# A hybrid decoder trunk whose list scheduler plays the program on another machine model

## The chip, the cores and the metric

The kernel runs on one core of a Trainium2 chip. The metric is device time in microseconds (us), the median of several runs. The engines are called as in the profile: PE is the tensor engine (PEld its weight loads), DVE the vector engine, ACT the scalar engine, POOL the GpSimd engine, SP the engine that issues most transfers.

## The reference

Two layers work on x of 256 tokens by 2048 features, in float32. A layer computes (cut from the reference):

```
h = rmsnorm(x, norm_mix[l])
fq, fk, fv, ff, gq, gk, gv, gg, gr, lg, lx = split(h @ w_in[l])        # 2048 x 5144
fox = softmax attention, 8 heads of 64, causal, with a cumulative forget bias from ff; then rmsnorm
gla = gated linear attention, 4 heads, chunked, decay from gr; rmsnorm per head, times silu(gg)
lru = rg_lru(causal_depthwise_conv(lx)) * gelu(lg); then rmsnorm
x = x + concat([fox, gla, lru]) @ w_out[l]                             # 2048 x 2048
h = rmsnorm(x, norm_ffn[l])
x = x + (silu(h @ w_gate[l]) * (h @ w_up[l])) @ w_down[l]              # 2048 x 5632 twice, 5632 x 2048
```

At the end one more rmsnorm gives the output, again 256 x 2048.

## The kernel before

Every product with a weight matrix is done in split form: a weight block of 128 x 1024 lands in a buffer `raw` (three of 1 MB), ACT casts it to the high part `wh` (L217 or L262), DVE subtracts to get the low part `wl` (L218 or L263), and PE multiplies high by high, high by low and low by high. There are four `wh` and four `wl` buffers, so the casts can run a few blocks ahead. `group` (L173 on) computes with tokens on the partitions, with the products in L200, L201 and L203 and the last blocks in L191 to L193; it does the output projection, called op, and the down projection, called dn. `group_T` (L224 on) computes with features on the partitions, L239 for the 512-column product and L240 for the 256-column one; it does lx, lg, gqk, fq, fk and the gate and up projections, called gu. `sum_T` (L281, L282) brings a result of these out of PSUM. Six PSUM buffers hold the results, two more (`aux`) hold everything small: transposes `tp`, softmax scores `fs`, transposed probabilities `pp`, attention outputs `fo`.

The mixers are written as generators. While a projection runs over its blocks, after each block it calls `next(steps)`, which emits a step of the mixer whose inputs are ready: conv taps (L483), the scans (L505), the chunk levels of the gated linear attention (masked copies in L684), the norm of the recurrent branch (L774), the tables `nb00` (L796) and `ck1` (L797) of the forget bias. The softmax runs beside the output projection: PE scores `fs` (L821), DVE subtracts the bias and takes the maximum (L837, L840, L841), ACT takes exp (L843), PE flips (`pp`, L852), ACT copies (`pT`, L854), PE multiplies with the values (`fo`, L863), DVE divides (L867), ACT squares (L871), DVE and POOL make the norm (L154, L156), DVE scales (L873), PE transposes (`tp`, L165), and ACT and DVE write the parts of `mt0` (L169, L170). The output projection reads the four quarters of its input in the order `mt2`, `mt3` (recurrent branch), `mt1` (linear attention), `mt0` (softmax), so the softmax has three quarters of the first half of the projection to run beside. The `final` function at the end adds the last products (L402), squares (L421), multiplies by the gain (L422), and scales by the norm (L431 on ACT, L433 on DVE) before the output is stored.

What the program text says is not yet the order of the queues. A list scheduler takes all instructions with what each waits for, plays the program on a model of the machine, and at each point gives an engine the ready instruction of highest priority; priority is the order of the text, but for stretches marked `tc.high_priority()` (the casts) or `tc.high_priority(SOONEST)` (the `sum_T` evacuations and the additions to x). What comes out is one fixed queue for each engine, worked in order on the chip. Which instruction is "ready" at a point is decided by the times of the model alone, so another model gives other queues.

## Time and profile before

| | us |
|---|---|
| time, median of 3 runs | 2082.35 (2082.15 to 2082.68) |
| profiled execution, its own time | 2081.86 |
| span of the profiled execution | 2080.1 |
| PE busy | 2063.2 |
| DVE busy | 1339.7 |
| ACT busy | 1108.6 |
| POOL busy | 12.9 |

The span is the stretch that the profile covers; the time has the ends around it. "Busy" of PE is a share of time in which a matmul is in its pipeline by a model of their ends, so it says that PE is fed, and not that it is at its peak. The granted clock is given by the profile as a share of 2.4 GHz. Names in the rows are those of the program; `op<-wh,mt` reads: result op, from wh and mt.

### The profile page before, as it was taken

What the parts mean: (1) busy time and instruction counts of PE and PEld (TensorE: products, weight loads), DVE (VectorE), ACT (ScalarE), POOL (GpSimd) and SP (SyncE); (2) the same over time, 40 slices, a digit from 0 to 9 for tenths busy, and PEclk for the clock granted to TensorE, in tenths of its full rate; (3) what the DMA queues carried; (4) which work ended last, traced back from release to release, by engine and by line L of the source; (5) the groups of instructions that cost most, each with busy time, mean ns of one, the idle gap of its engine ahead of it and who ended that gap; (6) DMA issues with size and microseconds to landing.
All of it is one profiled execution on the core that took longest, in us unless ns stands there. A gap on an engine that the chain in (4) does not pass through costs nothing.

```text
span 2080.1 us, 30286 instructions
## 1 busy us (share of the span) xinstructions
PE 2063.2 (99%) x11948; PEld 1865.3 (90%) x11948; DVE 1339.7 (64%) x1770; ACT 1108.6 (53%) x1557; POOL 12.9 (1%) x20
## 2 busy tenths in 40 slices
PE   9999999999999999999999999999999999999998
PEld 7899888999998899998898998889999888999987
DVE  7887856666655465655578878666665555565654
ACT  6875555554543345544458665555455444554543
POOL 0000000000000000000000000000000000000000
PEclk9999999999999999999999999999999999999999
DMA  7456545666666666666665565566666666666664
GB/s 277 151 190 194 196 147 198 202 200 199 200 199 204 205 201 200 199 201 202 201 196 161 185 193 182 162 202 198 200 199 199 200 204 205 201 199 201 202 203 162
DMA packets 302702, 406.66 MB, mean 196 GB/s; under 512 B 12208, under 2 KB 196960, under 8 KB 302432
## 3 DMA queue, kind: packets, MB, share of 16 engines
q1 hardware_dynamic: 297808, 401.47, 59.3%
q10 hardware_dynamic: 4752, 3.26, 0.5%
q8 instruction: 93, 1.52, 0.3%
q14 instruction: 49, 0.40, 0.1%
HBM read 402.57 MB, written 2.11 MB: 195 GB/s over the span
## 4 chain that ended last, share of the span: by engine, by line
PE 93%; DVE 3%; ACT 2%; issue 1%; DMA 0%; SPq 0%; ACTq 0%; POOLq 0%; DVEq 0%
PE gu L239 30%; PE gu L240 15%; PE dn L203 7%; PE dn L200 7%; PE dn L201 7%; PE lx L239 3%; PE op L201 2%; PE op L200 2%; PE op L203 2%; PE lx L240 1%; PE fq L239 1%; PE lg L239 1%; PE fk L239 1%; PE gqk L239 1%; DVE wl L218 1%
## 5 line engine op out<-in xcount | busy, mean ns | idle before, releaser
L239 PE MATMUL gu<-x,wh 128*128 128x512 f32 x2816 | 914.4, 382 | 0.0
L263 DVE TENSOR_TENSOR wl<-raw,wh 128x1024 fp32r<-128x1024 f32 (+1 forms) x465 | 566.1, 1220 | 371.9 <-ACT wh L262 371.8
L240 PE MATMUL gu<-x,wl 128*128 128x256 f32 x2816 | 739.3, 273 | 0.0
L262 ACT CAST wh<-raw 128x1024 fp32r<-128x1024 f32 (+1 forms) x465 | 485.4, 1047 | 456.9 <-PE gu L239 364.1
L239 PEld LDWEIGHTS gu<-x,wh 128*128 128x128 f32 x2816 | 519.6, 189 | 64.8
L240 PEld LDWEIGHTS gu<-x,wl 128*128 128x128 f32 x2816 | 539.6, 192 | 9.3
L218 DVE TENSOR_TENSOR wl<-raw,wh 128x1024 fp32r<-128x1024 f32 (+2 forms) x288 | 352.5, 1226 | 274.0 <-ACT wh L217 273.8
L217 ACT CAST wh<-raw 128x1024 fp32r<-128x1024 f32 (+2 forms) x288 | 300.8, 1047 | 331.2 <-PE dn L203 207.3
L200 PE MATMUL dn<-wh,ht 128*128 128x512 f32 x632 | 239.9, 380 | 0.0
L201 PE MATMUL dn<-wl,ht 128*128 128x512 f32 x632 | 239.5, 379 | 0.0
L203 PE MATMUL dn<-wh,ht 128*128 128x512 f32 x632 | 188.0, 379 | 0.0
L201 PEld LDWEIGHTS dn<-wl,ht 128*128 128x128 f32 x632 | 119.5, 189 | 16.9
L203 PEld LDWEIGHTS dn<-wh,ht 128*128 128x128 f32 x632 | 119.4, 189 | 16.9
L200 PEld LDWEIGHTS dn<-wh,ht 128*128 128x128 f32 x632 | 119.5, 189 | 16.8
L281 ACT COPY half<-gu 128x256 f32<-128x256 f32 x176 | 65.3, 371 | 45.7 <-PE gu L239 41.2
L239 PE MATMUL lg<-xt,wh 128*128 128x512 f32 x256 | 87.5, 394 | 1.4 <-DVE lg L282 1.4
L239 PE MATMUL lx<-xt,wh 128*128 128x512 f32 x256 | 87.3, 394 | 1.1 <-DVE xt L170 1.1
L200 PE MATMUL op<-wh,mt 128*128 128x512 f32 x224 | 87.1, 389 | 0.0
L201 PE MATMUL op<-wl,mt 128*128 128x512 f32 x224 | 86.0, 384 | 0.0
L240 PE MATMUL lx<-xt,wl 128*128 128x256 f32 x256 | 68.5, 279 | 0.0
L240 PE MATMUL lg<-xt,wl 128*128 128x256 f32 x256 | 67.2, 273 | 0.0
L203 PE MATMUL op<-wh,mt 128*128 128x512 f32 x224 | 67.0, 380 | 0.0
(300 smaller groups left out, 2313.3 us busy)
## 6 DMA issues: line engine op xcount, KB each, us to landing
raw<-in_w_gate SPq DMA_DIRECT2D x176, 512.0 KB, 3.5
raw<-in_w_up SPq DMA_DIRECT2D x176, 512.0 KB, 4.5
raw<-in_w_down SPq DMA_DIRECT2D x176, 512.0 KB, 4.8
raw<-in_w_in SPq DMA_DIRECT2D x55, 1024.0 KB, 5.0
raw<-in_w_out SPq DMA_DIRECT2D x64, 512.0 KB, 4.8
raw<-in_w_in SPq DMA_DIRECT2D x17, 512.0 KB, 3.6
raw<-in_w_in SPq DMA_DIRECT2D x16, 528.0 KB, 3.7
raw<-in_w_in SPq DMA_DIRECT2D x16, 520.0 KB, 3.9
```

Of the source, the lines that this page charges most:

```text
L200: T.matmul(out, hi, turns(wh[:, c]), start=k == 0, stop=False)
L201: T.matmul(out, hi, turns(wl[:, c]), start=False, stop=False)
L203: T.matmul(inturn(ps[i][h][:, :segs[i][1]]), lo, turns(wh[:, c]), start=False, stop=k == nk - 1)
L217: A.copy(wh, raw[:, j:j + jn, :tot])
L218: V.tensor_tensor(wl, raw[:, j:j + jn, :tot], f(wh), op=ALU.subtract)
L239: both = lambda: T.matmul(ps[i].rearrange("p (a t u) -> p a t u", a=2, u=2), wh[:, c], turns(xk), start=k == 0, stop=k == KT - 1)
L240: low = lambda: T.matmul(inturn(ps[i][:, 0:S]), wl[:, c], turns(xk[:, 0]), start=False, stop=False)
L262: A.copy(wh[:, js], raw[:, rs, :])
L263: V.tensor_tensor(wl[:, js], raw[:, rs, :], f(wh[:, js]), op=ALU.subtract)
L281: A.copy(two(c), halves_of(ps[:, S:]))
```

## The change

One argument is added where the program is built: the scheduler plays the program on a model that keeps time lines, in place of the default model. What the kernel computes, its instructions, buffers and priorities are as before. Of PE's 11,730 rows 1,552 stand at another place, of DVE's 1,772 rows 364, of ACT's 1,492 rows 227, of SP's 725 rows 3, and of POOL's none.

```
-    with tile.TileContext(nc) as tc:
+    with tile.TileContext(nc, schedule_with_timeline_sim=True) as tc:
```

The first place is the softmax of layer 1 on PE. `fs_2889` and `fs_2890` are the last two score tiles, `op0_...` the four result tiles of the output projection, `mt3` and `mt1` its earlier inputs, `mt0` the softmax's result. Before, the scores are followed by products of the projection (24 rows stand where the dots are; 12 more follow between pp and fo, 24 between fo and tp, 12 between the tp):

```order
L203 MATMUL op0_0_1_1_2708<-wh_2873,mt3_109 128x512
L821 MATMUL fs_2889<-fk_2183,fq_2182 128x256
L821 MATMUL fs_2890<-fk_2183,fq_2182 128x256
L821 MATMUL fs_2889<-fk_2183,fq_2182 128x256
L821 MATMUL fs_2890<-fk_2183,fq_2182 128x256
L200 MATMUL op0_0_0_0_2705<-wh_2918,mt3_109 128x512
...
L852 MATMUL pp_2950<-cst_80,pt_2895 128x128 x4
L852 MATMUL pp_2957<-cst_80,pt_2905 128x128 x4
L200 MATMUL op0_0_0_0_2705<-wh_2967,mt1_2454 128x512
```

Now the same stretch of PE's queue, from the last product ahead of `fs_2890` to the last flip:

```order
L203 MATMUL op0_0_1_1_2708<-wh_3056,mt1_2454 128x512
L821 MATMUL fs_2890<-fk_2183,fq_2182 128x256 x2
L852 MATMUL pp_2950<-cst_80,pt_2895 128x128 x4
L852 MATMUL pp_2957<-cst_80,pt_2905 128x128 x2
L863 MATMUL fo_2983<-fv_1952,pT_2864 128x64 x2
L863 MATMUL fo_2983<-fv_1952,pT_2871 128x64 x2
L863 MATMUL fo_2983<-fv_1952,pT_2864 128x64 x2
L863 MATMUL fo_2983<-fv_1952,pT_2871 128x64 x2
L863 MATMUL fo_2983<-fv_1952,pT_2955 128x64 x2
L852 MATMUL pp_2957<-cst_80,pt_2905 128x128 x2
```

The products with `mt3` and `mt1` now all stand ahead of `fs_2890`; three more pairs of fo and eight transposes tp follow the rows shown, and then the first product with `mt0`. Before, 72 products stood between `fs_2890` and that product; now none does, and 7 stand between `fs_2889` and `fs_2890`.

The second place is DVE beside the projection fq of layer 1. `wl_2270` and `wl_2292` are the low parts of two of its weight blocks. Before:

```order
L797 TENSOR_TENSOR ck1_1966<-ck1_1966,cst_80 128x1024
L263 TENSOR_TENSOR wl_2270<-raw_2241,wh_2269 128x1024
L263 TENSOR_TENSOR wl_2292<-raw_2289,wh_2291 128x1024
L684 COPY_PREDICATED at_1642<-msk_85,gx_2210 128x256x2
L774 SCALAR_TENSOR_TENSOR mt2_108<-hs_110,vec_83,mt2_108 128x256 x4
```

Now, from the same addition to the same cast:

```order
L797 TENSOR_TENSOR ck1_1966<-ck1_1966,cst_80 128x1024
L263 TENSOR_TENSOR wl_2270<-raw_2241,wh_2269 128x1024
L774 SCALAR_TENSOR_TENSOR mt2_108<-hs_110,vec_83,mt2_108 128x256 x3
L796 TENSOR_TENSOR nb00_1968<-ck0_1965,cst_80 128x1024
L774 SCALAR_TENSOR_TENSOR mt2_108<-hs_110,vec_83,mt2_108 128x256
L684 COPY_PREDICATED at_1642<-msk_85,gx_2210 128x256x2
L774 SCALAR_TENSOR_TENSOR mt3_109<-hs_110,vec_83,mt3_109 128x256 x2
L263 TENSOR_TENSOR wl_2292<-raw_2289,wh_2291 128x1024
```

The second cast now stands behind six L774, the table nb00 (L796) and the two masked copies.

The third place is DVE beside the projection lg of layer 1: `lg0` is its result as it is brought out of PSUM, `xc` the conv taps, `hs` the scan. Before:

```order
L263 TENSOR_TENSOR wl_940<-raw_910,wh_939 128x1024
L505 SCALAR_TENSOR_TENSOR hs_110<-av_543,ti_542 128x256 x2
L263 TENSOR_TENSOR wl_969<-raw_966,wh_968 128x1024
L282 TENSOR_TENSOR lg0_869<-lg00_0_659,half_870 128x256
L282 TENSOR_TENSOR lg0_869<-lg00_1_660,half_873 128x256
L505 SCALAR_TENSOR_TENSOR hs_110<-av_543,ti_542 128x256 x2
```

Now:

```order
L263 TENSOR_TENSOR wl_940<-raw_910,wh_939 128x1024
L483 SCALAR_TENSOR_TENSOR xc_885<-xp_645,vec_83,xc_885 128x256 x2
L263 TENSOR_TENSOR wl_969<-raw_966,wh_968 128x1024
L282 TENSOR_TENSOR lg0_869<-lg00_0_659,half_870 128x256
L505 SCALAR_TENSOR_TENSOR hs_110<-av_543,ti_542 128x256 x3
L282 TENSOR_TENSOR lg0_869<-lg00_1_660,half_873 128x256
```

The first evacuation and the conv taps now stand ahead of the scans; before, two scans stood ahead of the first evacuation and the taps came behind the last one.

## Rows read from the trace of the kernel before

**Rows 1.** Busy times of the page: engine, us, share of the span, instructions.

```profile
PE 2063.2 (99%) x11948; PEld 1865.3 (90%) x11948; DVE 1339.7 (64%) x1770; ACT 1108.6 (53%) x1557; POOL 12.9 (1%) x20
```

**Rows 2.** Timeline of PE in the down projection: start us, length us, instruction.

```profile
2060.71 0.38 PE L192 MATMUL dn<-wl,ht 128*128 128x512 f32 x1
2060.93 0.38 PE L193 MATMUL dn<-wh,ht 128*128 128x512 f32 x1
```

**Rows 3.** PE's waits: line waited with <- line waited for: us, times, longest.

```profile
PE lg L239 <- DVE lg L282: 1.4, 2, 0.7
PE gp L490 <- DVE xc L483: 1.4, 2, 0.7
...
PE gqk L239 <- DVE gz L581: 0.7, 2, 0.3
PE ga L200 <- DVE lg L282: 0.6, 2, 0.3
```

**Rows 4.** Windows: stretch, length, busy PE PEld DVE ACT POOL, PEclk, DMA, GB/s.

```profile
3.83:7.25 3.42, 2.05 (x11) 0.94 (x9) 0.39 (x1) 0.99 (x2) 0.00 (x0) 1.00 1.00 331
7.25:14.07 6.82, 6.07 (x20) 5.14 (x21) 3.92 (x8) 3.25 (x6) 0.00 (x0) 0.50 1.05 404
...
273.90:304.00 30.10, 30.10 (x166) 26.54 (x166) 16.58 (x38) 14.43 (x25) 0.55 (x1) 1.00 0.44 147
2071.60:2075.70 4.10, 0.00 (x0) 0.00 (x0) 2.38 (x6) 2.06 (x4) 0.54 (x1) 1.00 0.46 162
```

**Rows 5.** Timeline of the softmax beside the output projection, layer 1.

```profile
273.98 1.14 PE L821 MATMUL fs<-fk,fq 64*128 64x256 f32 x8
...
275.16 1.23 DVE L218 TENSOR_TENSOR wl<-raw,wh 128x1024 fp32r<-128x1024 f32 x1 [2.24 <-ACT wh L217]
...
276.31 0.28 DVE L837 CUSTOM_DVE_ANT_0 pt<-fs,ck 128x128 f32<-128x128 f32 x1
...
277.36 0.16 DVE L840 TENSOR_TENSOR mx<-mx 128x2 f32<-128x2 f32 x1
...
277.90 0.51 ACT L843 ACTIVATE pt<-pt,mx 128x256 f32<-128x256 f32 x1 [2.77 <-DVE mx L841]
...
280.33 1.09 PE L852 MATMUL pp<-cst,pt 128*128 128x128 f32 x8
...
281.76 1.05 ACT L854 COPY pT<-pp 128x512 f32<-128x512 f32 x2
...
283.84 3.68 PE L863 MATMUL fo<-fv,pT 128*128 128x64 f32 x32
...
287.56 0.69 DVE L867 TENSOR_TENSOR on<-fo,rs 128x512 f32<-128x512 f32 x1 [1.17 <-PE fo L863]
...
289.86 0.49 DVE L873 TENSOR_SCALAR on<-on,rf 128x512 f32<-128x512 f32 x1 [0.67 <-POOL rf L156]
...
292.60 0.60 PE L165 MATMUL tp<-cst,on 128*128 128x128 f32 x4
...
293.79 0.47 ACT L169 ACTIVATE mt<-tp,vec 128x256 fp32r<-128x256 f32 x1
```

**Rows 6.** Timeline of DVE beside fq, layer 1, and of PE there.

```profile
210.70 2.35 DVE L263 TENSOR_TENSOR wl<-raw,wh 128x1024 fp32r<-128x1024 f32 x2
212.97 1.32 DVE L684 COPY_PREDICATED at<-msk,gx 128x512 f32<-128x512 uint8 x1
214.07 1.65 DVE L774 SCALAR_TENSOR_TENSOR mt<-hs,vec,mt 128x256 fp32r<-128x256 f32 x4
...
215.70 0.38 PE L239 MATMUL fq<-xt,wh 128*128 128x512 f32 x1
...
220.58 1.27 DVE L796 TENSOR_TENSOR nb<-ck,cst 128x1024 f32<-128x1024 f32 x1
```

**Rows 7.** Timeline of ACT and DVE at the end of the kernel.

```profile
2068.83 1.33 ACT L431 ACTIVATE y<-y,rfin 128x512 f32<-128x512 f32 x2 [1.09 <-POOL rfin L156]
2068.84 0.88 DVE L433 TENSOR_SCALAR y<-y,rfin 128x512 f32<-128x512 f32 x2 [0.72 <-POOL rfin L156]
```

## The prediction

> **What bounds the kernel now.** I read the busy shares first. TensorE (PE) is busy for 2063.2 of 2080.1 us and no other engine passes 64% [rows 1]; two 512-column matmuls start 0.215 us apart (2060.93 less 2060.71) though each is shown with 0.38 us [rows 2], so the end of one, 0.16 us, is drawn over the start of the next, and a wait shown for PE hides 0.16 us more. The kernel is one PE queue that almost never stops. An order of the same instructions can therefore win only what PE waits now, and can lose whatever the new order leaves uncovered. Second, PE's list of waits: behind the start of the program four lines make nearly all of it, each twice, once a layer, 1.4, 1.4, 0.7 and 0.6 us [rows 3]. Third, the windows, for the granted clock: in the stretch from 3.83 us, where PE had been busy for 2.05 of 3.42 us, the clock was 1.00 (2.4 GHz); in the 6.82 us behind it, it was 0.50 (1.2 GHz). The last rows of the group show 30.10 us busy of 30.10 around the softmax, and an idle 4.10 us near the end with the clock still 1.00 [rows 4]. Last the timeline of the softmax, of fq and of the end [rows 5 to 7]. The profiled execution took 2081.86 us, 0.5 under the median of 2082.35; the sum is made against 2081.86.
>
> **Waits that go.** Before, a scan or a weight cast stood ahead of the evacuations (L282) and conv taps (L483) for which lg, gp, gqk and ga wait. The new order of VectorE (DVE) puts the taps and the first evacuation ahead of scans and casts. If all four go, the visible 4.1 us go, and 8 times 0.16 us hidden in the drawn ends: 5.4. I take all of it, **-5.4**; the bounds are -5.4 and 0 (other DVE work stands ahead of other steps now).
>
> **fq, once a layer.** Before, DVE made wl_2270 and wl_2292 back to back, done at 210.70 + 2.35 = 213.05; PE comes to the step that takes wl_2292 at 215.70, with 2.65 us to spare [rows 6]. In the new order six L774 (1.65/4 = 0.41 each), the nb00 addition L796 (1.27) and the two L684 (1.10 to the start of the next) stand between the two casts: 6 x 0.41 + 1.27 + 1.10 = 4.8 us, so wl_2292 is ready at about 217.8. PE can first do four L239 (0.87 us) of that step, up to 216.6: it waits 1.3 us, **+2.6** for two layers. Behind the waiting matmul PE's whole queue stands. Low bound 0, if PE comes there later; high bound 1.9 a layer, +3.8, if ck0's transfer makes L796 wait a further 0.6 us.
>
> **The softmax tail, once a layer, which decides.** Before, 72 matmuls of the output projection (15.5 us at 0.215) stand in PE's queue in four blocks between the last score matmuls (fs_2889, fs_2890) and the first matmul that reads mt0, the softmax's result. They cover the whole chain of exp, flip, attend, norm and transpose: PE is busy all through [rows 4, 5]. In the new order only 7 (1.5 us) stand behind fs_2889 and **none** behind fs_2890; its whole chain lies bare. From the durations in [rows 5]: fs_2890 0.57 (half of 1.14); four L837 at 0.21 (five starts from 276.31 to 277.36), 0.84; the cast L218 that now stands between these and the maximum, 1.14 to 1.23; L840 and L841, 0.32; the first exp, 0.51; two transposes pp, 0.27 (1.09/8 each); ten fo matmuls, which now stand ahead of the last two pp, 2.30 (3.68/16 each); two pp, 0.27; the copy pT, 0.52; six fo, 1.38; from `on` at 287.56 to the end of its scaling at 290.35, 2.79; three transposes tp, 0.45 (0.60/4 each); the evacuation L169, 0.47. Together 11.8; six crossings between PE and another engine at about 0.1 (287.52 to 287.56 is the shortest, 281.42 to 281.76 the longest, in which ACT was partly busy) make 12.4 us. In that time PE has fs 0.57, eight pp 1.09, all fo 3.68 and eight tp 1.2, which is 6.5 us. It stands idle for 12.4 - 6.5 = 5.9 us, **+11.8** for two layers. The work that follows has nothing to catch up with, since PE is the bound. Bounds: +8 if casts are not in the way and crossings cost nothing (4.2 a layer), +16 if ACT's casts or a late fs_2890 add 2 us a layer.
>
> **The clock behind the tail.** In the tail PE would be busy for about 6.5 of 12.4 us; at the start it had been busy for 2.05 of 3.42 us when the clock fell to 0.50 for 6.82 us [rows 4]. The rows show no other place where PE works and waits by turns, so I take the start as the nearest. If the tail too is followed by one such stretch at half rate, PE does in it what takes 3.4 us at full rate: 3.4 us lost a layer, **+6.8**. Bounds: 0 (the clock stayed through the idle 4.10 us near the end), and +14 if the half rate falls on the tail itself, whose 5.2 us of PE steps in the chain (0.57 + 0.54 + 3.68 + 0.45) then take twice as long, on top of part of the stretch. I take the middle, being nearer to the row at the start.
>
> The Trainium skill (TensorE: Matmul & The Clock Gate, "Part 1: The HAM clock gate") says that half rate is the default, to which the gate returns once the engine has been idle for a while. In the tail PE is never idle for long (about 3 us at most, from `on` to tp), so by that rule the clock would stay and this term would be 0. The row at the start, half rate behind a stretch in which PE was mostly busy, does not agree; the rule's result is rival (a).
>
> **Start and end.** At the start two casts (2.35 us for a pair, [rows 6] has the same form) now stand between the evacuations L170 of xt01, and again single casts among those of xt02 and xt03; they free the PSUM buffers for which the next transposes wait. PE is partly idle there [rows 4]: I take less than half of two such pairs, **+2.0**, with -2 and +4.7 as bounds, as earlier casts can also feed lx sooner. At the end two L431 and two L433 of the first half (1.33 on ACT, 0.88 on DVE, [rows 7]) now stand ahead of the last square and the last L422 of the other half: between the two, **+1.1** (0 to +1.3). The rest of what moves, casts and steps among each other in the long stretches of gate, up and down, costs nothing as DVE and ACT have a third to half of their time free [rows 1]; if that cover went, a cast of 1.2 us would show as a PE wait on wl.
>
> **Sum.** 2081.9 - 5.4 + 2.6 + 11.8 + 6.8 + 2.0 + 1.1 = 2100.8, 0.9% above before; set beside the median it is 2101.3. I forecast **2101**. A measurement of this kernel tells 0.2%, 4 us, from no change.
>
> **Rivals.**
> (a) The tail is bare but the clock stays at 2.4 GHz: 2100.8 - 6.8 = 2094. For it: the idle 4.10 us at 1.00. Against: the start.
> (b) More falls: the clock drops inside the tail and fq's L796 waits: 2100.8 + 7.2 + 1.2, and the start at its bound, 2.7 more: 2112.
> (c) The change doesn't do on the chip what its order says: PE, which takes its rows in order, reaches fs_2890 late enough, or its chain early enough, that only the small terms are left, -5.4 + 2.6 + 2.0 + 1.1: 2082. It would take 6 us of work between fs_2890 and the last pp, which PE's rows don't have.
> (d) The other side, faster: the tail is covered. If single links of the chain run beside PE's own 6.5 us of softmax work and not after it (the fo matmuls of the first heads while the last are still flipped), the tail needs no more than those 6.5 us. DVE's new order must then serve PE at fq and at the start too: 2081.9 - 5.4 + 1.1 and at best -2 at the start, 2076. It decides from an idle time under about 0.9 us a layer (2 us, to stay under 2078). Against it: fo, the norm and the transposes follow each other by data, and the cast stands in DVE's queue; the links add to 12.
>
> **How the numbers follow.** Forecast 0.60 (2096 to 2108), (a) 0.22 (2090 to 2096), (b) 0.10 (2108 to 2116), (c) 0.05, (d) 0.03. The range 2090 to 2112 leaves out (c), (d) and half of (b), 0.13, and the edges of the rest, some 0.05 more. Faster by over 0.2%: 0.03. Within 0.2%: 0.05. Slower: 0.92.
>
> **What would show it.** In the new profile PE's waits should hold, twice each, lines that are not there now: pp waiting for ACT's exp (L843), fo for the copy (L854), tp for DVE's scaling (L873), op for ACT's mt0 (L169), with some 6 us a layer near 285 to 300 and a thousand us later, and fq waiting for DVE L263 with about 1.3 us each. lg, gp, gqk and ga should be gone from the list. The windows behind the two tails should show a granted clock of 0.50 for some 7 us; if it is 1.00, (a) holds. I am wrong if PE's idle time in the softmax is under 3 us a layer, or if a wait that I haven't named (wl in gate and up, or a transfer) is the longest of the list.

## The result and the profile after

The changed kernel takes 2101.39 us (median of 5 runs, 2100.95 to 2101.78), against 2082.15 (2080.57 to 2082.68) for the kernel before in the same measurement: a ratio of 1.0099, with a 95% interval of 1.0088 to 1.0109. The prediction was 2101. The profiled execution took 2100.95 us with a span of 2099.1, 19.0 us more than before. The total agrees with the sum to a fifth of a microsecond, but its terms don't: the tail cost 25.4 us and not 18.6, and the rest gave 6.4 and not cost 0.3.

PE's waits in the changed kernel (line waited with <- line waited for: us in total, times, longest), which answer to [rows 3]:

```profile
PE pp L852 <- ACT pt L843: 4.7, 4, 2.0
PE tp L165 <- DVE on L873: 3.4, 2, 1.7
PE fo L863 <- ACT pT L854: 1.3, 2, 0.7
PE tp L165 <- DVE rx0s L338: 1.3, 1, 1.3
PE tp L165 <- issue: 1.2, 1, 1.2
...
PE tp L165 <- DVE on L867: 1.1, 2, 0.6
PE lx L239 <- DVE xt L170: 0.9, 1, 0.9
```

lg, gp, gqk and ga are gone. Four new lines are the links of the softmax chain, twice each or four times, 10.5 us together; two (rx0s and issue) are of the start. Of the four links that the prediction named three are there; op waiting for ACT's mt0 (L169) is not, and tp waiting for the division (L867) is new. fq is not there.

The timeline of the tail in layer 1 (start us, length us, instruction, [idle before <- releaser]) answers to [rows 5]:

```profile
282.69 1.13 PE L821 MATMUL fs<-fk,fq 64*128 64x256 f32 x4
...
285.46 1.13 PE L821 MATMUL fs<-fk,fq 64*128 64x256 f32 x4
...
287.31 0.44 PE L852 MATMUL pp<-cst,pt 128*128 128x128 f32 x2 [0.36 <-ACT pt L843]
287.47 1.22 DVE L218 TENSOR_TENSOR wl<-raw,wh 128x1024 fp32r<-128x1024 f32 x1
...
289.71 0.44 PE L852 MATMUL pp<-cst,pt 128*128 128x128 f32 x2 [1.97 <-ACT pt L843]
...
289.99 4.15 PE L863 MATMUL fo<-fv,pT 128*128 128x64 f32 x20
...
295.24 2.83 PE L863 MATMUL fo<-fv,pT 128*128 128x64 f32 x12 [0.68 <-ACT pT L854]
...
301.00 1.54 PE L165 MATMUL tp<-cst,on 128*128 128x128 f32 x6 [1.68 <-DVE on L873]
...
302.47 0.80 PE L200 MATMUL op<-wh,mt 128*128 128x512 f32 x1
303.05 0.63 PE L201 MATMUL op<-wl,mt 128*128 128x512 f32 x1
```

From the last score tile at 285.46 to the first product with mt0 at 302.47 are 17.0 us. Every link stands where the order put it, the cast among them. But the 32 fo, 3.68 us before, take 6.98 here, and the first products with mt0 0.63 instead of 0.38. The windows of that stretch (stretch, length, busy PE PEld DVE ACT POOL, granted clock, DMA, GB/s) say why; the fourth is the tail of layer 2, the last two are the start, and answer to [rows 4]:

```profile
285.46:290.22 4.76, 2.43 (x14) 1.57 (x14) 2.35 (x12) 3.48 (x10) 0.00 (x0) 1.00 0.27 86
290.22:307.29 17.07, 14.14 (x52) 11.87 (x52) 3.35 (x8) 3.12 (x7) 0.55 (x1) 0.50 0.17 60
307.29:320.00 12.71, 12.71 (x62) 11.12 (x61) 7.50 (x9) 7.63 (x10) 0.00 (x0) 1.00 0.29 87
1327.87:1344.94 17.07, 12.86 (x50) 11.10 (x51) 3.88 (x11) 4.21 (x11) 0.55 (x1) 0.50 0.20 62
3.83:7.25 3.42, 3.05 (x11) 1.58 (x9) 0.33 (x1) 0.98 (x3) 0.00 (x0) 1.00 1.01 326
7.25:14.07 6.82, 6.01 (x39) 5.46 (x40) 4.54 (x9) 4.42 (x9) 0.00 (x0) 1.00 1.03 390
```

The clock fell to 1.2 GHz 4.8 us into the tail, when PE had been busy for 2.43 of these 4.76 us, and came back 4.8 us after the first product with mt0. In layer 2 it fell 3.0 us into the tail (from 1324.90 to 1327.87), when PE had been busy for 1.93 of 2.97 us. At the start, where it was 0.50 before, it stayed at 2.4 GHz.

Where the time went is read by setting the same instructions of the two traces side by side (their start, in us of the span):

| instruction | before | after | later by |
|---|---|---|---|
| layer 1: first gv | 179.36 | 175.23 | -4.1 |
| layer 1: first fk | 228.88 | 224.72 | -4.2 |
| layer 1: first gate/up, behind the output projection | 349.62 | 358.50 | +8.9 |
| layer 2: last lx | 1086.51 | 1095.39 | +8.9 |
| layer 2: last gv | 1233.24 | 1238.51 | +5.3 |
| layer 2: last fk | 1280.91 | 1286.19 | +5.3 |
| layer 2: first gate/up | 1379.62 | 1397.27 | +17.7 |
| last matmul | 2070.93 | 2088.29 | +17.4 |
| span | 2080.1 | 2099.1 | +19.0 |

Two steps of 13.0 and 12.4 us lie between fk and gate/up, that is in the output projection with its softmax; the mixers of layer 2 gain 3.6; the end loses 1.7.

### The profile page after: what moved, and what is told of

The parts are those of the page before. It is cut to its first block, busy times and chain, and to the rows that moved or that the text cites. A ratio compares the mean times of both kernels' runs of the same rounds, so it can differ in the third digit from the quotient of the medians.

```text
span 2099.1 us, 30296 instructions
## 1 busy us (share of the span) xinstructions
PE 2073.3 (99%) x11948; PEld 1874.5 (89%) x11948; DVE 1345.5 (64%) x1770; ACT 1108.9 (53%) x1557; POOL 11.7 (1%) x20
## 4 chain that ended last, share of the span: by engine, by line
PE 97%; DMA 1%; DVE 1%; ACT 1%; issue 0%; POOL 0%; ACTq 0%; POOLq 0%
PE gu L239 29%; PE gu L240 15%; PE dn L200 6%; PE dn L203 6%; PE dn L201 6%; PE lg L239 3%; PE op L200 2%; PE op L201 2%; PE op L203 2%; PE lx L239 2%; PE fk L239 1%; PE gqk L239 1%; PE lg L240 1%; PE fq L239 1%; PE lx L240 1%; PE fo L863 1%
## 5 line engine op out<-in xcount | busy, mean ns | idle before, releaser
L218 DVE TENSOR_TENSOR wl<-raw,wh 128x1024 fp32r<-128x1024 f32 (+2 forms) x288 | 352.5, 1227 | 278.1 <-ACT wh L217 276.6
L239 PE MATMUL lx<-xt,wh 128*128 128x512 f32 x256 | 82.8, 385 | 0.9 <-DVE xt L170 0.9
L372 ACT CAST ht<-u 128x512 fp32r<-128x512 f32 x44 | 27.1, 617 | 70.4 <-DVE u L370 70.4
```

What stands on the lines that cost most here:

```text
L218: V.tensor_tensor(wl, raw[:, j:j + jn, :tot], f(wh), op=ALU.subtract)
L239: both = lambda: T.matmul(ps[i].rearrange("p (a t u) -> p a t u", a=2, u=2), wh[:, c], turns(xk), start=k == 0, stop=k == KT - 1)
L372: A.copy(hts[-1][:, 0, js, :], u)
```

## The experiments

Each kernel is named with its edit. Where PE's order is written by hand, the first half of the output projection stands in a region in which PE issues what the text emits in the order of the text, `group` asks for the next step after each 6 products instead of 12, and a table says behind how many products a softmax step stands; DVE, ACT and SP remain the scheduler's. The text sets their priority, so their softmax steps move along with PE's; no run changes PE's order with theirs held. Line numbers lie a few lines further down in these kernels (L855 for L852, L846 for L843, L866 for L863).

**cover_new: the changed kernel, tail covered.**

```
-            ps = group(KT, mixed, ..., steps=steps)
+            with tc.manual_schedule(engines={PE}) if g == 0 else nullcontext():
+                ps = group(KT, mixed, ..., steps=steps, fine=g == 0)
+            plan = {18: pairs(0), 36: flips(0), 42: flips(1), 48: pairs(2), 54: attend(0), 60: flips(2, 3),
+                    72: pairs(4), 96: flips(4, 5), 108: attend(1), 132: split(0), 144: split(2)}
```

> The changed kernel (queues made with time lines), but PE's order of the first half of the output projection is written by hand, so that 72 products stand between the last scores and the first product with mt0 in four blocks, as before the change; DVE, ACT and SP are left to the new scheduling. Theory (the bare softmax tail on PE is the whole loss, 13.0 and 12.4 us in the two traces; the rest of the new order gains 4.2 and 3.6 us and loses 1.7 at the end): 2101.4 - 25.4 = about 2076, under the kernel before. Rival 1 (the order of DVE and ACT around the softmax makes the loss, PE's order only follows it): it stays at about 2101. Rival 2 (the gain elsewhere is only apparent, since the tail gives PE's feeders time to run ahead): about 2082.

Measured 2079.17 us (10 runs, 2077.55 to 2080.35), 0.9991 of the kernel before (0.9982 to 1.0000). Some 21 us of the loss are gone (19.2 us over the kernel before became 1.9 under it, each against its own measurement) with PE's order written by hand and the rest left to the new scheduling, so rival 1 falls as it was stated. In its trace the first gv stands 4.2 us earlier than before, and between layer 2's lx and gv 3.6 us more are won, the figures of the changed kernel; so the gain in the mixers is real, and rival 2 falls. Of the 3 us short of the forecast the trace shows 2.1 in the two output projections, most of it fo of the first queries, which waits 0.7 us a layer for DVE, with 0.16 more hidden in the drawn end; the profiled execution (2077.62) was also 1.5 under the median. The end loses 1.7, as in the changed kernel and as the forecast had it. The window that held 30.10 busy us before holds 29.99, at full clock:

```profile
273.90:304.00 30.10, 29.99 (x162) 26.30 (x161) 16.38 (x30) 15.49 (x28) 0.55 (x1) 1.00 0.49 159
```

**cover_old: the kernel before, same order by hand.**

> The kernel before (default scheduling) with the same order written by hand for PE in the first half of the output projection. A control: theory and both rivals expect 2082, within 3 us; what it is off by is the price of writing the order by hand.

Measured 2086.48 (6 runs), 1.0027 (1.0015 to 1.0039): 5 us over the kernel before, so the hand-written order is not free under the default scheduling, and the 3 us allowed for it were too few. Its trace puts 2.7 us a layer into the output projection, where PE waits for an exp and, ahead of the first fo, for DVE's maxima:

```profile
PE pp L855 <- ACT pt L846: 2.5, 2, 1.2
PE fo L866 <- DVE mx L840: 1.7, 2, 0.8
```

**bare_old: the kernel before, tail bare.**

```
+            plan = {18: pairs(0), 66: flips(0), 72: flips(1), 96: pairs(2), 114: (attend(0), flips(2)),
+                    138: (flips(3), unit(4)), 144: (unit(5), flips(4, 5), attend(1), split(0), split(2))}
```

> The kernel before (default scheduling) with one part of the change done alone: PE's order of the first half of the output projection is written by hand as the changed kernel has it, 6 products behind the first of the last two score tiles and none behind the second. Theory: 2082 + 25.4 = 2107, and a stretch of some 17 us at half clock behind each tail. Rival 1 (DVE's and ACT's order makes the loss): 2082 to 2086. Rival 3 (the tail costs its idle time only, and the clock follows something else, as the start): about 2082 + 2 x 6.7 = 2095, with the clock at 1.00.

Measured 2104.56 (4 runs, 2104.12 to 2106.84), 1.0115 (1.0098 to 1.0132). Its trace has 12.9 and 11.8 us more than before in the two output projections, and at most 0.3 us elsewhere: 24.7 of the 25.4 us of the changed kernel, made under the old scheduling by PE's order in the softmax and the DVE and ACT steps that follow it. Rivals 1 and 3 fall. What writing by hand costs here is small: the last score tile starts 39.0 us into the projection, in the changed kernel 38.5. Of DVE's own order the chain of the tail holds one cast, L218 with 1.22 us of the 17.0 above. The clock falls in both tails:

```profile
290.00:294.30 4.30, 2.38 (x11) 1.11 (x9) 2.69 (x13) 2.82 (x7) 0.00 (x0) 1.00 0.12 45
294.30:311.37 17.07, 13.88 (x54) 12.46 (x55) 3.38 (x8) 3.99 (x11) 0.56 (x1) 0.50 0.18 61
1338.78:1352.43 13.65, 10.92 (x46) 9.98 (x45) 3.17 (x7) 2.99 (x7) 0.56 (x1) 0.50 0.13 48
```

**fill_old and fill_less: the bare tail with work for PE.**

```
+            plan = {..., 144: (unit(5), idle_work(12), flips(4, 5), attend(1), idle_work(12), split(0), split(2), idle_work(2))}
+            def idle_work(n):   # fill_less: 9, 9, 1
+                for _ in range(n):
+                    T.matmul(pts["w"], mt[2][:, 0, 0, 0:P], mt[2][:, 0, 0:2, :], start=True, stop=True)
```

> As bare_old, and PE does 26 more matmuls a layer (128x512 on data at hand, their results unused) at the places where it would wait in the tail: 12 behind the last scores, 12 behind fo, 2 behind the transposes. At 0.215 us they are 5.6 us of work, laid into waits of about 3, 3 and 0.5 us. Theory (about half of the tail's loss is the clock, which falls as PE waits by turns): the clock stays at 1.00, and the time is bare_old less about 2 x 6 us, near 2095. Rival (the clock falls for another reason, or its loss is nothing): no faster than bare_old, or slower by up to 11 us.

> The kernel before with PE's order as in bare_old and fewer matmuls at the places of PE's waits: 9, 9 and 1 a layer in place of 12, 12 and 2, 1.5 us less. In fill_old PE had no wait left in the tail, so its 26 may be more than the waits hold. Theory: the clock stays at 1.00, the tail costs its idle time alone, about 6 us a layer, and the time is fill_old's 2096 less 2 x 1.4 = 2093, with small waits back in the list. Rival (the tail without its clock loss is 7.4 us long, as in fill_old): 2096. If 19 are too few to hold the clock: up to 2104.

fill_old: 2096.03 (4 runs, 2094.39 to 2097.74), 1.0075 (1.0060 to 1.0090). fill_less: 2095.77 (4 runs, 2094.34 to 2096.49), 1.0077 (1.0060 to 1.0093). More work for PE makes the kernel 8.5 us faster, because the clock stays; in fill_less, from the start of the fill behind the last scores:

```profile
288.28:307.29 19.01, 17.09 (x98) 14.49 (x98) 7.00 (x20) 7.93 (x19) 0.55 (x1) 1.00 0.17 56
```

A tail costs 7.4 us in fill_old's trace (both layers) and 7.6 in fill_less's, against 12.9 and 11.8 in bare_old's. So 4 to 5.5 us of a tail are the clock and at most 7.4 to 7.6 are the idle time with all else that the bare order costs. That fill_less gained nothing on fill_old was a miss: its waits came back as the fill left (pp 2.3 and tp 1.4 in its list of waits), so the 26 had filled what was idle and lengthened nothing. Both traces also show a start without half clock (2.3 and 2.8 us earlier at the first gv than before), so the gain in median, which runs over several executions, is the safer figure.

**warm_old: the kernel before, all warm-up matmuls first.** The program begins with eight matmuls on zeros whose results are unused (L106). The changed kernel has them all first, too; before, the eighth stood behind four transposes.

```
+    with tc.high_priority(SOONEST):
         for _ in range(WARM):
             T.matmul(wp, warm[:, 0, 0:P], warm[:, 0, 0:512], start=True, stop=True)
```

> The kernel before with one part of the change done alone: all eight warm-up matmuls stand ahead of PE's first transposes, where before the eighth stood behind four of them. cover_old and fill_old have the same queues up to the softmax; one ran the start with a stretch of half clock and the other without, and came 2.4 us earlier to gv. Theory 1 (the place of the eighth matmul decides whether the clock falls at the start): the clock is 1.00 from the start, and the time 2079 in every execution. Theory 2 (it is chance from one execution to the next): the times spread as those of the kernel before, 2079 to 2082.5.

Measured 2079.24 (10 runs, 2079.04 to 2082.12), 0.9997 (0.9988 to 1.0007). Seven executions lie at 2079.0 to 2079.6 and three at 2080.7 to 2082.1; of the kernel before, 9 of 25 lie under 2079.5. It is not in every execution, so theory 1 falls as stated; whether the order makes the good case more frequent is left open by these numbers. In its profiled execution the start ran at 1.00 and the first gv came 2.8 us earlier, with nothing else changed. The 2.8 us are about what a half-rate stretch at the start costs, and with the same queues up to the softmax it comes and goes: before, cover_old and bare_old had it in their profiled executions, fill_old and fill_less did not.

**best_a, best_b, best_c: toward a version that beats both.** best_a is cover_new with fo and most of what follows it 6 products later and with DVE and ACT in written order in the final norm; best_b has the first block in written order as well; best_c is best_a with PE in written order in the last group of the down projection.

```
 best_a:  plan = {18: pairs(0), 36: flips(0), 42: flips(1), 48: pairs(2), 60: attend(0), 66: flips(2, 3),
+                 78: pairs(4), 102: flips(4, 5), 114: attend(1), 138: split(0), 144: split(2)}
+         with tc.manual_schedule(engines={DVE, Activation}):
              final(ps, g, r2)
 best_b:  with tc.manual_schedule(engines={DVE, Activation}) if l == 0 else nullcontext():
              ps = proj_T(O_LX, ...)
 best_c:  with tc.manual_schedule(engines={PE}) if end and g else nullcontext():
              ps = group(..., f"dn{l}_{part}_{g}", ...)
```

> As cover_new (new scheduling, PE's order of the output projection by hand), with fo of the first half of the queries one half block later (in cover_new it waited 0.7 us a layer), and with DVE and ACT in written order in the final norm, as before the change. Theory: 2079.2 less 2 x 0.8 less 1.7 at the end = about 2076. If the end's loss in the changed kernel isn't the order of DVE and ACT there: 2077.5.

> As best_a, and DVE and ACT also work the first block of the program (the first half of lx in layer 1) in written order, so that the evacuations of the transposes stand ahead of the next casts, as before the change. Theory (the new order stalls the start by about 2 us, hidden in the traces by a clock that did not fall): 2074. Rival (the start is no worse in the new order): 2076, as best_a.

> As best_a, and PE works the last group of the down projection in written order, too: in the changed kernel the last 48 matmuls of the four results stand mixed, so that the first half's results are done 3 us before the last matmul instead of 4.8, and best_a left the end 2.8 us longer than before. Theory (PE's order at the end, with DVE's and ACT's, is the end's loss): 2078.0 less 2.8 = 2075.2, 0.25% under the kernel before. Rival (the end hangs on the last stores, which end when they end): 2078, as best_a.

best_a took 2077.99 (10 runs), 0.9990 (0.9981 to 0.9999). The tail is better (the output projections cost 0.1 us a layer over the kernel before), but the expectation for the end was wrong: from the start of the last matmul to the end of the span are 11.9 us, 2.8 more than before. best_b took 2078.15 (10 runs), the same: written order at the start gains nothing, since PE then waits for x itself (4.1 us in its list). best_c took 2074.66 (7 runs, 2074.44 to 2075.98), 0.9973 (0.9961 to 0.9984), as its theory said: what best_a lost at the end was PE's order (9.1 us from the last matmul's start, as before). PE's order there was not put back by itself. best_c is faster than the kernel before by 0.27%, and than the changed one by some 25 to 27 us (they were timed in two measurements).

## Why the prediction was right, and which steps were not

**Waits that go: right in place, too small.** -5.4 was forecast. In layer 2, where the start plays no part, the mixers gain 3.6 us, 7.2 for two layers if layer 1 gains the same: 2.0 up to lg's end, 0.6 each in ga and gqk, 0.5 in fv. The list of waits names no fv before, so its 0.5 us a layer were not to be seen there.

**fq: wrong.** +2.6 was forecast, and nothing was lost (-4.1 at gv, -4.2 at fk). DVE and PE in the changed kernel, answering to [rows 6]:

```profile
205.31 1.20 DVE L263 TENSOR_TENSOR wl<-raw,wh 128x1024 fp32r<-128x1024 f32 x1
...
211.02 1.21 DVE L263 TENSOR_TENSOR wl<-raw,wh 128x1024 fp32r<-128x1024 f32 x1
211.56 1.03 PE L239 MATMUL fq<-xt,wh 128*128 128x512 f32 x4
212.43 0.61 PE L240 MATMUL fq<-xt,wl 128*128 128x256 f32 x4
```

The second cast ends at 212.23, 0.2 us ahead of the product that needs it. What stands between the casts is 4.6 us, near the 4.8 forecast. The step that failed took the time of the first cast from the old trace: the new order had moved earlier work, so that DVE made it 5.4 us sooner than before (205.31 against 210.70) and PE came only 4.1 sooner (211.56 against 215.70). The 1.3 us between the two are the forecast wait.

**The softmax tail: right in mechanism and in idle time, PE's own work too small.** +11.8 was forecast for the idle time. The list of waits has ten in the two tails, 10.5 us, and 0.16 us under each drawn end makes 12.1. The filled tails, at full clock, cost more, about 15 (7.4 to 7.6 a layer). The chain was sized well: in fill_less, at full clock, it runs from 287.23 (last scores) to 300.72 (first product with mt0), 13.5 us, against 12.4. The term that was mis-sized is fs_2890, taken as half of 1.14 [rows 5]. In the old order the two score tiles alternate, and 8 records take 1.14 us together. In the new order each tile stands alone and its 4 records take 1.13. The two heads of an alternating pair lie in opposite halves of the 128 rows of fq and fk, and their records start in pairs 7 ns apart in the trace of before (273.978 and 273.985), each 0.38 us long or more: they ran beside each other. Apart they cost 0.5 us more for each tile, 2.1 us in the two layers, which the prediction put at nothing. No run changed this by itself, and some 1 us of the 15 stays open. The Trainium skill (TensorE: Matmul & The Clock Gate, "Part 3: Packing small matmuls — row/col tiling") says that matmuls on different groups of rows overlap, which agrees with 8 records in 1.14 us.

**The clock: it fell as forecast, but earlier and for longer.** +6.8 was forecast, from one stretch of 6.82 us behind each tail. It fell inside the tail, as rival (b) had it, and lasted 17.07 us in each layer, so that fo, transposes and the first products ran at half rate, too. The rest of rival (b), fq and a worse start, did not come. The changed kernel's tails cost 25.4 us together; less 7.4 to 7.6 each for a tail at full clock (of bare_old's order) leaves about 10. No wait in the list is longer than 2.0 us, and the clock fell all the same, so rival (a) falls. The rule of the Trainium skill (TensorE: Matmul & The Clock Gate, "Part 1: The HAM clock gate"), as the prediction read it, would have kept the clock up here; the trace does not agree. Another section of that page, "A second HAM failure mode: psum-queue depth-cycling", tells of a kernel in which many small idle times between groups of matmuls made the clock swing; that is nearer to this tail, and the prediction should have weighed it. PE's work by turns with waits went ahead of the fall here, and matmuls laid into the waits kept the clock up; what decides the moment of the fall is not shown.

**Start: right sum of stalls, wrong net.** +2.0 was forecast; the two new waits of the start sum to 2.5 us. But before's profiled execution had a half-rate stretch at the start and after's had none. Layer 1's -4.2 up to fk, less the 3.6 of waits, leaves -0.6 for the start as a whole, within a microsecond of 2.5 of stalls less the 2.3 to 2.8 us that the stretch costs. The prediction took the clock of the start as it was found in one execution.

**End: near in size, half the reason.** +1.1 was forecast from ACT and DVE; 1.7 came. In the changed kernel DVE's first addition waits for PE:

```profile
2085.26 1.41 DVE L402 SCALAR_TENSOR_TENSOR x<-dn,r,x 128x512 f32<-128x512 f32 x2 [4.61 <-PE dn L193]
...
2089.97 1.34 ACT L431 ACTIVATE y<-y,rfin 128x512 f32<-128x512 f32 x2 [1.23 <-POOL rfin L156]
2089.97 0.88 DVE L433 TENSOR_SCALAR y<-y,rfin 128x512 f32<-128x512 f32 x2
...
2091.21 0.61 ACT L421 ACTIVATE junk<-x 128x512 bf16<-128x512 f32 x1
```

L431 and L433 [rows 7] stand ahead of the last square and L422, as forecast, and the last square starts 2.9 us behind the last matmul's start (2091.21 less 2088.29), before 1.3. But PE mixes the last matmuls of the results, so that the first addition starts 3.0 us ahead of the last matmul's start (2088.29); before, two additions had begun by then, 7.1 and 4.8 us ahead of it. best_a put DVE and ACT back alone and the end did not shrink, as the forecast's reason would have it, but grew to +2.8; best_c put PE back as well and the end was 9.1 us long again. So the order of DVE and ACT costs what it does only with PE's.

So the forecast of the whole was right because the tail, which decided, was found and priced by the right mechanism, and because two errors cancelled: the tail cost 6.8 us more than its two terms (25.4 against 18.6), and waits, fq and start together 7.0 less than theirs (-7.8 against -5.4 + 2.6 + 2.0 = -0.8). Alone, either would have moved the forecast by 7 us; that they cancel, and that the total comes out to 0.2 us, is luck.

## What to carry to other kernels

Where one engine is full, look in a new order for the place where its long queue of independent work runs out ahead of a serial chain; count what stands behind the last instruction that starts the chain. Price such a bare chain twice: by its idle time, and by the clock at which the engine's own pieces of it and what follows run. A wait computed from an old trace's times holds only if the order ahead of it is unchanged, and what comes and goes, such as the clock of the start, has to be looked up in more than one execution.

## What the runs showed of the hardware

- PE's clock fell to half (1.2 GHz) where PE worked and waited by turns, with no wait over 2.0 us ahead of the fall: after 2.43 busy us of 4.76 and 1.93 of 2.97 in the changed kernel's two layers, after 2.38 of 4.30 in bare_old's first. It stayed at full rate where 19 unused matmuls a layer were laid into the waits, and the kernel became some 8.5 us faster by doing more (2104.56 to 2095.77, with 26 matmuls to 2096.03).
- The same queues ran the first 15 us at full clock in some profiled executions (fill_old, fill_less) and with 6.8 us at half clock in others (before, cover_old, bare_old); the first gv came 2.3 and 2.8 us earlier than before where the clock stayed.
- Score matmuls of 64 rows took 1.14 us for 8 records where two tiles in opposite halves of the rows alternate, and 1.13 us for 4 where one tile's stood alone.
